# Input rows of token groups 1 to 3 scaled in a channel-by-token layout instead of being transposed on TensorE, and a reordered start of the kernel

## The chip, the cores and the metric

The kernel runs on one core of one Trainium2 chip. The core's engines run their own instruction streams in order and wait for each other through semaphores: TensorE (PE in the profile, with PEld for its weight loads), VectorE (DVE), ScalarE (ACT), GpSimd (POOL) and SyncE (SP). DMA transfers are issued from the streams of SP, ACT and POOL. The metric is the time of one execution on the device in microseconds (us), lower is better. Before the change it is 1321.57 us, the median of 3 runs (1318.48 to 1323.26).

## The reference, cut to what matters

One layer of an encoder, 2048 tokens of width 1024, all in float32. The change touches only the first two lines: the modulated RMS norm that makes `h`, and the part of the input projection that is computed first.

```
c_act = silu(c)
shift, scale, gate = split(c_act @ w_ada + b_ada, 3)
h = rmsnorm(x, norm_w) * (1 + scale) + shift          # x: 2048 tokens x 1024 channels
proj = h @ w_in + b_in                                # 1024 -> 4624 columns
...                                                   # 2-D neighbourhood attention, bidirectional mLSTM
out = rmsnorm(x + gate * (mixed @ w_out), final_norm_w)
```

For one token `t` and one channel `d` this is `h[t, d] = x[t, d] * r[t] * g[d] + s[d]`, where `r[t]` is the reciprocal root of the mean square of the token's row, `g` is `norm_w * (1 + scale)` and `s` is `shift`.

## The kernel before

The tokens are worked on in four **groups** of 512 (`NG`, `GT`), a group in four tiles of 128 tokens. The channels are eight **slices** of 128 (`KT`, index `k`). TensorE contracts over the partitions, so `h` has to lie with channels on the partitions and tokens along the free dimension: tile `hhi[g][:, k, :]` for the high part in fp32r and `hlo[g][:, k, :]` for what that rounding leaves over. Every product is made of three: high by high, high by low and low by high (`mm3`, lines 560 to 562).

The input `x` comes as rows of tokens. `square` (line 253) sums the squares of a row on ScalarE, `roots` makes `r` with a few small VectorE steps, `scale_x` multiplies the row tile by it, and TensorE transposes the 128x128 pieces into PSUM (`turned` for group 0, line 357; `make_h` for groups 1 to 3, line 372). From PSUM, `make_h` makes the high part on ScalarE (line 374), the full value on VectorE (line 376) and the low part on GpSimd (line 377).

All this stands in `start` (with `vo_first` and `vo_group`, which it calls) under a manual schedule: each engine runs its instructions in the order in which the code emits them. The order is:

1. **The front.** Loads of group 0's rows, of the conditioning vector spread over 128 partitions (`cb`, 512 KB), of modulation weights (`load_mod`) and of projection weights (`load_p`). TensorE runs 20 products on constants (`dense`, line 329), which serve nothing but keeping it busy. Then it makes `g` and `s` of slice 0 (line 349); those of the other slices are dot products on VectorE (`mod`, line 257).
2. **The k loop** over the eight slices of group 0. For each, ScalarE makes the high part and the full value (`first_h`, line 364), VectorE the low part (line 365) and the next slice's two dot products, and TensorE runs 24 products (`products`, line 392) into `firsts` (block 0, four PSUM banks of the pool `pp`) and `seconds` (block 1, two banks). In the last two slices ScalarE also squares group 1's rows, and a third block's weights are split into `w_extra` (lines 212 and 213).
3. **Evictions and block 2 of group 0.** `vo_group` adds the bias on VectorE while it copies a PSUM bank to a staging tile (line 632), takes a sigmoid of one half on ScalarE (line 638) and stores the tile to DRAM (`d_ck`, lines 641 and 643). There are two staging tiles, used in turn, so the third call needs the store of the first to have landed.
4. **Groups 1 to 3**: `vo_first(g)` runs block 0 slice by slice (line 615, 12 products of 272 columns per slice, 96 in all) into the four banks of `pp`, and `vo_group(1, 1, g)` then runs block 1, 24 products of 256 columns for each of the four token tiles.

Between the token tiles of such a `vo_group` stands `next(self.chain)`, which emits the next group's preparation: after the third tile's eviction (o = 2) come slices 0 and 1 of `make_h`, after the fourth's (o = 3) slices 2 and 3, then slice 4; slices 5 to 7 follow the first three slices of the next `vo_first`:

```
def next_h(tiles):
    yield
    yield
    for k in (0, 2):
        make_h(tiles, k)
        make_h(tiles, k + 1)
        yield
```

## Time and profile before

| | |
|---|---|
| median of 3 runs | 1321.57 us |
| the profiled execution's own time | 1321.6 us |
| its span, first to last instruction | 1319.8 us |
| mean granted TensorE clock | 0.993 of full speed |
| bytes moved | 257.59 MB, 195 GB/s over the span |
| first product of the projection | 18.11 us |
| first eviction of block 0: groups 1, 2, 3 | 78.81, 105.77, 132.71 us |

A row of the timeline gives the start, the duration, the engine, the source line, the operation and its tiles; in brackets stands how long the engine had been idle and what ended that. Rows with xN are N instructions merged, from the first's start to the last's end. A row of windows gives each engine's busy time in a stretch (and its instructions in parentheses), then the granted TensorE clock, the busy share of the DMA engines and their rate. A TensorE product in float32 shows as two instructions. Matmuls overlap in their pipeline, so the distance from one start to the next is what a product costs, not its duration. Everything the change touches lies in the first 135 us.

### The profile page before, as it was taken

The page shows a single profiled execution, that of the slowest core. Times are in us where ns is not written, and L with a number is a line of the kernel's source. Part 1 is how long each engine was busy: PE and PEld are TensorE (multiplying, and loading weights), DVE is VectorE, ACT ScalarE, POOL GpSimd, SP SyncE. Part 2 cuts the span into 40 slices and gives each one's busy share as a digit, 9 for nine tenths or more (in the row PEclk, how much of TensorE's full clock was granted, in tenths as well). Part 3 has the DMA queues.
Part 4 walks back from the last instruction along what each step waited for, and adds up shares of the span by engine and source line. Part 5 has one row for each costly group of instructions (what it writes and reads, how often), then busy time and mean ns, then how long its engine had stood idle before and what let it go on. Part 6 is the DMA issues. An engine that isn't in the chain of part 4 may idle for free.

```text
span 1319.8 us, 23211 instructions
## 1 busy us (share of the span) xinstructions
PE 1287.2 (98%) x8244; PEld 1106.7 (84%) x8244; DVE 784.7 (59%) x2418; ACT 540.4 (41%) x1175; POOL 223.6 (17%) x279
## 2 busy tenths in 40 slices
PE   9899999999999999999999999999999999999996
PEld 8899999999888787888888888888777778778785
DVE  6754542113456577266778788777547676666663
ACT  5543423543313423123323333333356555465561
POOL 0044102442000000111222002121211211112211
PEclk9999999999999999999999999999999999999999
DMA  9967966999276786445757766746789877868871
GB/s 363 338 165 210 259 157 155 227 236 226 77 185 174 181 210 175 143 137 166 210 149 209 236 175 205 234 152 185 208 254 237 204 199 189 187 169 194 194 186 48
DMA packets 235237, 257.59 MB, mean 195 GB/s; under 512 B 30950, under 2 KB 192102, under 8 KB 235122
## 3 DMA queue, kind: packets, MB, share of 16 engines
q1 hardware_dynamic: 150174, 183.10, 49.8%
q0 software_dynamic: 20496, 36.21, 11.3%
q10 hardware_dynamic: 64452, 36.80, 10.0%
q8 instruction: 65, 1.06, 0.3%
q14 instruction: 50, 0.41, 0.1%
HBM read 171.51 MB, written 92.72 MB: 200 GB/s over the span
## 4 chain that ended last, share of the span: by engine, by line
PE 80%; DMA 8%; DVE 5%; issue 3%; ACT 2%; POOL 0%; ACTq 0%; SPq 0%; DVEq 0%; POOLq 0%
PE pq L1003 21%; PE y L1582 11%; PE pc L560 4%; PE pc L561 4%; PE pc L562 4%; PE pvo L560 3%; PE pvo L562 3%; PE pvo L561 3%; PE pT L1522 3%; DMA tab<-d_t 3%; PE pO L1537 3%; PE pvo L615 3%; PE pv L562 2%; PE pv L561 2%; PE pv L560 2%
## 5 line engine op out<-in xcount | busy, mean ns | idle before, releaser
L1003 PE MATMUL pq<-hhi,whi_a 128*128 128x512 f32 x512 | 208.2, 407 | 0.8 <-ACT u L908 0.8
L1003 PE MATMUL pq<-hlo,whi_a 128*128 128x512 f32 x512 | 208.3, 407 | 0.0
L1003 PE MATMUL pq<-hhi,wlo_a 128*128 128x512 f32 x512 | 206.7, 404 | 0.0
L1003 PEld LDWEIGHTS pq<-hhi,whi_a 128*128 128x128 f32 x512 | 96.8, 189 | 17.7 <-ACT u L908 1.3
L1003 PEld LDWEIGHTS pq<-hhi,wlo_a 128*128 128x128 f32 x512 | 96.8, 189 | 16.4
L1003 PEld LDWEIGHTS pq<-hlo,whi_a 128*128 128x128 f32 x512 | 96.7, 189 | 16.0 <-issue 0.5
L1524 ACT ACTIVATE pt<-pT 96x384 f32<-96x384 f32 (+3 forms) x128 | 65.9, 515 | 88.2 <-PE pT L1522 85.3
L1503 ACT ACTIVATE pbuf<-pbuf,mn 128x480 f32<-128x480 f32 (+5 forms) x128 | 76.1, 596 | 51.7 <-DVE mn L1502 51.5
L977 POOL TENSOR_TENSOR wlo_a<-rawq,whi_a 128x1024 fp32r<-128x1024 f32 x19 | 45.5, 2397 | 290.2 <-ACT whi_a L976 276.8
L1582 PE MATMUL y<-hhi,whi_a 128*128 128x512 f32 x256 | 91.3, 418 | 1.0 <-ACT whi_a L1552 1.0
L1582 PE MATMUL y<-hhi,wlo_a 128*128 128x512 f32 (+1 forms) x272 | 91.6, 403 | 0.2 <-ACT y L1589 0.2
L1502 DVE CUSTOM_DVE_ANT_0 pbuf<-pS,tab 128x480 f32<-128x480 f32 (+5 forms) x128 | 63.2, 540 | 39.6 <-PE pS L1494 33.0
L1247 ACT ACTIVATE num<-px,gtile 128x129 f32<-128x129 f32 x120 | 38.3, 366 | 113.8 <-PE px L1242 86.2
L1522 PEld LDWEIGHTS pT<-ident,pbuf 128*128 128x128 f32 (+2 forms) x416 | 51.2, 137 | 28.7 <-issue 8.7
L1522 PE MATMUL pT<-ident,pbuf 128*128 128x128 f32 (+2 forms) x416 | 67.7, 276 | 7.2 <-DVE pbuf L1514 5.7
L1266 POOL TENSOR_TENSOR hm<-hm,ck 128x128 f32<-128x128 f32 x64 | 26.5, 414 | 255.2 <-DVE hm L1265 229.5
L632 DVE TENSOR_TENSOR stvo<-pvo,brow 128x256 f32<-128x256 f32 x60 | 24.9, 423 | 75.3 <-PE pvo L562 57.2
L560 PE MATMUL pvo<-whi_b,hhi 128*128 128x256 f32 x224 | 63.8, 285 | 0.0
L850 ACT ACTIVATE dec<-dec,gtile 128x128 f32<-128x128 f32 x128 | 42.7, 394 | 50.5 <-POOL dec L843 44.6
L562 PE MATMUL pvo<-whi_b,hlo 128*128 128x256 f32 x224 | 63.0, 281 | 0.0
L561 PE MATMUL pvo<-wlo_b,hhi 128*128 128x256 f32 x224 | 63.0, 281 | 0.0
L1582 PEld LDWEIGHTS y<-hhi,wlo_a 128*128 128x128 f32 x272 | 48.7, 191 | 9.0 <-issue 2.4
(331 smaller groups left out, 3374.3 us busy)
## 6 DMA issues: line engine op xcount, KB each, us to landing
ck<-d_ck SPq DMA_DIRECT2D x64, 384.5 KB
rawq<-in_w_main_dram SPq DMA_DIRECT2D x28, 512.0 KB
raw<-in_w_main_dram SPq DMA_DIRECT2D x18, 512.0 KB
kv<-d_ck SPq DMA_DIRECT2D x64, 128.5 KB
dec<-d_mneg SPq DMA_DIRECT2D x32, 256.0 KB
d_ck<-dec ACTq DMA_DIRECT2D x32, 256.0 KB
d_qna<-qst ACTq DMA_DIRECT2D x32, 256.0 KB
xr<-in_x_dram POOLq DMA_DIRECT2D x15, 512.0 KB, 8.6
```

Of the source, the lines that this page charges most:

```text
L560: nc.tensor.matmul(ps, lhi(k), rhi(k), start=(k == 0), stop=False)
L561: nc.tensor.matmul(ps, lhi(k), rlo(k), start=False, stop=False)
L562: self.mark = nc.tensor.matmul(ps, llo(k), rhi(k), start=False, stop=(k == KT - 1))
L615: self.nc.tensor.matmul(self.firsts[o][:, :272], h, (hi, lo, hi)[n][:, k, :], start=(k == 0 and n == 0), stop=(k == KT - 1 and n == 2))
L850: nc.scalar.activation(t[:, o, :], t[:, o, :], AF.Exp, bias=self.cols["g"][:, d, h, c : c + 1])
L977: (eng or nc.gpsimd).tensor_tensor(lo[:, :, cs], raw, hi[:, :, cs].bitcast(F32), ALU.subtract)
L1003: self.mark = nc.tensor.matmul(patch_ps(ps) if patch else ps, w, self.htok(h, g, k, patch), start=(k == 0 and n == 0), stop=(k == KT - 1 a ...
L1502: nc.vector.tensor_tensor_reduce(pt[:, :nk], ps, tabs[place[u]][j][:, :nk], 1.0, 3e38, ALU.add, ALU.min, mn)
L1503: nc.scalar.activation(pt[:, :nk], pt[:, :nk], AF.Exp, bias=mn, scale=-1.0, accum_out=sums[:, j : j + 1])
L1522: nc.tensor.transpose(ps[:cs, i, :], U[u][j][:, i * cs : (i + 1) * cs], self.ident)
L1524: nc.scalar.activation(t[:cs, :nch, :], ps[:cs, :nch, :], AF.Copy)
L1582: nc.tensor.matmul(y, m[:, k, :], w[k][:, cs], start=(k == 4 and n == 0), stop=(k == 3 and n == 2))
```

## The change

**Groups 1 to 3.** The host hands over a second copy of `x`, `x_t`, laid out by group, channel within the slice, slice, token. `make_h` no longer transposes: `load_t` brings the group's channels straight in. The rows are still loaded, for their sums of squares only, so 6 MB are read in addition. The factor `r[t]`, which now runs along the free dimension, is spread over all partitions by `spread`: four small VectorE steps put it on diagonals, and four float32 products with a matrix of ones (128 columns each) write it to a PSUM bank. A slice of `h` is then a VectorE step (x by `g` by the bank), ScalarE's high part with the shift, and a VectorE step for the low part; GpSimd has no part in it.

**The front.** The conditioning vector is loaded as one row on ScalarE's queue, ahead of its three small loads; ScalarE takes its silu, TensorE spreads it with two float32 products of 512 columns and ScalarE copies it out. These two products stand ahead of the constant ones, which are now 14, with 3 and 2 more around the second half of the sums for slice 0. Group 0's rows are scaled in two pieces. The modulation weights are loaded earlier.

**The end of the k loop.** The last slice's products run bank by bank, group 1's rows are loaded in slice 6 instead of slice 2 and squared after the loop instead of within it, and the first two tiles of block 2 of group 0 go to two banks of another pool (`tops`).

```
@@ start
-            nc.sync.dma_start(t, self.x[tt * P : (tt + 1) * P, :])
+        def load_t(g):
+            held = self.hpools[g + 1].tile([P, 4, D], F32, tag=f"hhi{g + 1}", name=f"xt_{g}") if g < 3 else None
+            for j in range(4):
+                t = x_tile(f"xt_{g}_{j}") if held is None else held[:, j, :]
+                nc.sync.dma_start(t, self.x_t[g, :, 2 * j : 2 * j + 2, :].rearrange("p k t -> p (k t)"))
+                for i in range(2):
+                    xc[g, 2 * j + i] = t[:, i * GT : (i + 1) * GT]
...
+        def spread(tiles, rst):
+            diag = xp.tile([P, GT], F32, tag="h", bufs=2, name=f"diag_{tiles[0]}").rearrange("p (j q) -> p j q", j=4)
+            for j in range(4):
+                nc.vector.tensor_scalar(diag[:, j, :], self.ident, rst[:, j : j + 1], None, ALU.mult)
+            ps = self.tq.tile([P, GT], F32, tag="tb", name=f"rb_{tiles[0]}")
+            def run():
+                for j in range(4):
+                    nc.tensor.matmul(ps[:, j * P : (j + 1) * P], self.ones, diag[:, j, :], start=True, stop=True)
+            return ps, run
...
+        crow = ada.tile([1, D], F32, name="crow")
+        nc.scalar.dma_start(crow, self.c_row)
-        nc.sync.dma_start(cb, self.c_row.broadcast_to([P, D]))
...
-        for _ in range(20):
-            nc.tensor.matmul(dense[:, :240], self.ident, self.big, start=True, stop=True)
+        nc.scalar.activation(crow, crow, AF.Silu)
+        for j in range(2):
+            cbs.append(self.tq.tile([P, GT], F32, tag="tp", name=f"cb_{j}"))
+            nc.tensor.matmul(cbs[j], self.ones[0:1, :], crow[:, j * GT : (j + 1) * GT], start=True, stop=True)
+        warm(14)
...
         def make_h(tiles, k):
-            tp = self.tq.tile([P, GT], F32, tag=("tp", "tb")[k % 2], name=f"tp_{tiles[0]}_{k}")[:, :n]
-            for j, tt in enumerate(tiles):
-                nc.tensor.transpose(tp[:, j * P : (j + 1) * P], xt[tt][:, k * P : (k + 1) * P], self.ident)
-            nc.scalar.activation(hi, tp, AF.Identity, bias=self.shT[:, k : k + 1], scale=self.gT[:, k : k + 1])
-            nc.vector.tensor_scalar(h, tp, self.gT[:, k : k + 1], self.shT[:, k : k + 1], ALU.mult, ALU.add)
-            nc.gpsimd.tensor_tensor(lo, h, hi.bitcast(F32), ALU.subtract)
+            nc.vector.scalar_tensor_tensor(h, xc[g, k], self.gT[:, k : k + 1], spreads[g], ALU.mult, ALU.mult)
+            nc.scalar.activation(hi, h, AF.Identity, bias=self.shT[:, k : k + 1])
+            nc.vector.scalar_tensor_tensor(lo, h, self.shT[:, k : k + 1], hi.bitcast(F32), ALU.add, ALU.subtract)
...
         def products(k):
             turns = [(b, o, n) for ns in ((0, 1), (2,)) for b in range(2) for o in range(4) for n in ns]
+            if k == KT - 1:
+                turns.sort()
...
-        def next_h(tiles):
+        def next_h(tiles, run):
             yield
+            run()
             yield
             for k in (0, 2):
...
-                self.vo_group(2, 2, 0, brow=brow)
+                tops = [self.tq.tile([P, GT], F32, tag="tp", name=f"pvo_2_{o}") for o in range(2)]
+                self.vo_group(2, 2, 0, brow=brow, tops=tops)
```

Three places show how instructions move. The first is VectorE's order where group 2 is prepared during block 1 of group 1: `pvo` are the banks being evicted to the staging tile `stvo`, `h` and `hlo` the slices made for group 2. Before:

```order
L632 TENSOR_TENSOR stvo_1_994<-pvo_6_1049,brow_130 128x2x128
L376 TENSOR_SCALAR h_0_1081<-tp_0_1075,gT,shT 128x512
L376 TENSOR_SCALAR h_1_1090<-tp_1_1084,gT,shT 128x512
L632 TENSOR_TENSOR stvo_1_994<-pvo_7_1093,brow_130 128x2x128
L376 TENSOR_SCALAR h_2_1125<-tp_2_1119,gT,shT 128x512
```

The same place now:

```order
L672 TENSOR_TENSOR stvo_1_993<-pvo_6_1052,brow_130 128x2x128
L406 SCALAR_TENSOR_TENSOR h_0_1078<-xt_650,gT,rb_992 128x512
L408 SCALAR_TENSOR_TENSOR hlo_954<-h_0_1078,shT,hhi_953 128x512
L406 SCALAR_TENSOR_TENSOR h_1_1082<-xt_650,gT,rb_992 128x512
L408 SCALAR_TENSOR_TENSOR hlo_954<-h_1_1082,shT,hhi_953 128x512
L672 TENSOR_TENSOR stvo_1_993<-pvo_7_1086,brow_130 128x2x128
L406 SCALAR_TENSOR_TENSOR h_2_1112<-xt_650,gT,rb_992 128x512
L408 SCALAR_TENSOR_TENSOR hlo_954<-h_2_1112,shT,hhi_953 128x512
```

The low part of a slice, which was GpSimd's, now stands on VectorE between the full value of its slice and that of the next, and it reads `hhi`, which ScalarE makes from that full value in between.

The second place is the start of TensorE's stream, up to the first transpose. Before:

```order
L329 MATMUL dense<-big,ident 128x240 x20
L349 MATMUL mod_251<-cact,mod_hi 128x1 x16
L357 MATMUL tp_0_270<-ident,x_164 128x128
L357 MATMUL tp_0_270<-ident,x_166 128x128
L357 MATMUL tp_0_270<-ident,x_168 128x128
```

The same place now:

```order
L356 MATMUL cb_198<-crow,ones 128x512
L356 MATMUL cb_200<-crow,ones 128x512
L350 MATMUL dense<-big,ident 128x240 x14
L381 MATMUL mod_252<-cact,mod_hi 128x1 x8
L350 MATMUL dense<-big,ident 128x240 x3
L381 MATMUL mod_252<-cact,mod_hi 128x1 x8
L350 MATMUL dense<-big,ident 128x240 x2
L392 MATMUL tp_0_278<-ident,x_166 128x128
```

TensorE's first instruction now needs ScalarE's silu of the row `crow`, and five constant products stand inside the sums for slice 0.

The third place is ScalarE's order from the end of the k loop to the first store of a staging tile (`junk` are the squares of group 1's rows). Before:

```order
L253 ACTIVATE junk_550,ssq_284<-xs_383 128x1024
L253 ACTIVATE junk_552,ssq_284<-xs_383 128x1024
L212 ACTIVATE w_extra<-raw_0_344 128x1024
L364 ACTIVATE hhi_102<-tp_7_537,shT,gT 128x512
L364 ACTIVATE h_7_580<-tp_7_537,shT,gT 128x512
L253 ACTIVATE junk_584,ssq_284<-xs_383 128x1024
L253 ACTIVATE junk_586,ssq_284<-xs_383 128x1024
L212 ACTIVATE w_extra<-raw_1_511 128x1024
L638 ACT_TABLE_LOAD
L638 ACTIVATE stvo_0_635<-stvo_0_635 128x4x128
L641 DMA d_ck<-stvo_0_635 128x4x257
```

The same place now:

```order
L212 ACTIVATE w_extra<-raw_0_353 128x1024
L399 ACTIVATE hhi_102<-tp_7_541,shT,gT 128x512
L399 ACTIVATE h_7_588<-tp_7_541,shT,gT 128x512
L212 ACTIVATE w_extra<-raw_1_515 128x1024
L260 ACTIVATE junk_630,ssq_629<-x_554 128x1024
L260 ACTIVATE junk_632,ssq_629<-x_556 128x1024
L260 ACTIVATE junk_634,ssq_629<-x_558 128x1024
L260 ACTIVATE junk_636,ssq_629<-x_560 128x1024
L678 ACT_TABLE_LOAD
L678 ACTIVATE stvo_0_660<-stvo_0_660 128x4x128
L681 DMA d_ck<-stvo_0_660 128x4x257
```

All four squares now stand between the second weight split and the table load ahead of the first sigmoid and its store.

130 lines of the change are left out of this document (71 added, 59 removed).

## The prediction

> **What bounds the kernel now.** I read the page's totals and chain first, then windows over the changed part, then its timeline. TensorE is the bound:
>
> ```profile
> span 1319.8 us, 23211 instructions
> PE 1287.2 (98%) x8244; PEld 1106.7 (84%) x8244; DVE 784.7 (59%) x2418; ACT 540.4 (41%) x1175; POOL 223.6 (17%) x279
> ...
> PE 80%; DMA 8%; DVE 5%; issue 3%; ACT 2%; POOL 0%; ACTq 0%; SPq 0%; DVEq 0%; POOLq 0%
> ```
>
> ```profile
> 20.00:30.00 10.00, 9.62 (x79) 9.26 (x77) 9.74 (x16) 4.83 (x8) 0.00 (x0) 0.99 1.03 404
> 40.00:50.00 10.00, 7.83 (x60) 7.17 (x58) 6.94 (x12) 9.58 (x15) 0.00 (x0) 1.00 0.90 327
> 50.00:60.00 10.00, 8.70 (x62) 8.73 (x63) 6.83 (x26) 4.24 (x5) 0.00 (x0) 0.83 0.97 336
> 90.00:100.00 10.00, 10.00 (x86) 10.00 (x85) 6.16 (x9) 5.22 (x8) 8.09 (x7) 1.00 0.87 238
> ```
>
> Columns: PE, PEld, DVE, ACT, POOL, clock, DMA. In the k loop (20 to 30) VectorE is as full as TensorE, 9.74 of 10. Around 50 TensorE idles and its clock falls. From 60 on it is never idle. So taking TensorE work out of groups 1 to 3 pays only while the engines that feed it keep up, and whatever the third group's end is shifted by, the 98% busy remainder passes on. I therefore follow three marks, the first eviction of block 0 in groups 1, 2 and 3:
>
> ```profile
> 78.81 0.43 DVE L632 TENSOR_TENSOR stvo<-pvo,brow 128x256 f32<-128x256 f32 x1 [4.71 <-PE pvo L615]
> ...
> 88.49 0.43 DVE L632 TENSOR_TENSOR stvo<-pvo,brow 128x256 f32<-128x256 f32 x1 [2.42 <-PE pvo L562]
> ...
> 105.77 0.43 DVE L632 TENSOR_TENSOR stvo<-pvo,brow 128x256 f32<-128x256 f32 x1 [4.71 <-PE pvo L615]
> ...
> 132.71 0.43 DVE L632 TENSOR_TENSOR stvo<-pvo,brow 128x256 f32<-128x256 f32 x1 [4.71 <-PE pvo L615]
> ```
>
> A group takes 26.95 us, all of it TensorE issuing.
>
> **Groups 2 and 3: what goes and what comes.** Gone are 32 transposes a group:
>
> ```profile
> 92.01 1.47 PE L372 MATMUL tp<-ident,xs 128*128 128x128 f32 x12
> 93.24 0.37 PE L615 MATMUL pvo<-whi_a,hhi 128*128 128x272 f32 x1
> ```
>
> Twelve of them hold the next product off by 1.23, and it settles 0.09 later: 0.11 each, 3.5 us a group. Added are four float32 products of 128 columns. The constant products, 240 columns and two records each, give the rate:
>
> ```profile
> 1.50:6.20 4.70, 4.63 (x12) 3.94 (x13) 1.00 0.95 329
> 6.60:12.40 5.80, 5.73 (x29) 5.03 (x27) 1.00 0.97 331
> ```
>
> That is 0.40 a record at first and 0.20 later, so 0.11 for 128 columns: eight records, 0.9, with weight loads 1.0 us. If nothing waited, a group would gain 2.5.
>
> But VectorE now runs full value, low part, full value, low part, and each low part waits for ScalarE's high part of the same slice, which waits for the full value. VectorE takes its instructions in order, so a slice costs a whole round:
>
> ```profile
> L945 DVE SCALAR_TENSOR_TENSOR acc_k<-u,cw,acc_k 128x512 f32<-128x512 f32 x64 | 45.5, 747 | 0.4
> ...
> L1038 DVE SCALAR_TENSOR_TENSOR qst<-pq,bcol,qst 128x512 fp32r<-128x512 f32 x24 | 17.9, 747 | 18.4 <-ACT qst L1037 18.4
> ...
> L947 ACT ACTIVATE acc_k<-acc_k,cb 128x512 f32<-128x512 f32 x16 | 11.6, 722 | 12.8 <-DVE acc_k L945 12.8
> ...
> L299 ACT ACTIVATE whi_a<-raw 128x512 fp32r<-128x512 f32 x4 | 2.5, 629 | 0.7 <-DMA raw<-in_w_main_dram 0.7
> ...
> 157.28 1.41 DVE L529 SCALAR_TENSOR_TENSOR gsum<-ga,cact,gsum 128x512 f32<-128x512 f32 x2
> ```
>
> The fused step of 512 columns takes 0.747, from SBUF (L945) or with a PSUM operand (L1038); two in a row start 0.66 apart (L529). ScalarE from SBUF takes 0.63 as a plain copy and 0.72 with a bias column, which is this case. The hand-over costs 0.03 (45.53 + 0.77 to 46.33, below). Round: 0.75 + 0.03 + 0.72 + 0.03 + 0.66 = **2.2 us**, bounds 2.1 and 2.3. TensorE eats a slice of block 0 in 1.5 (12 products 0.125 apart). Before, GpSimd took the low parts and kept ahead:
>
> ```profile
> 101.14 1.30 POOL L377 TENSOR_TENSOR hlo<-h,hhi 128x512 fp32r<-128x512 f32 x1 [0.44 <-DVE h L376]
> ```
>
> Its last low part ended 13.95 after the third eviction (88.49), in good time for the last slice. Now: third eviction 0.34, two rounds 4.4, fourth eviction 0.34 (it waits behind those rounds, and the next block needs its bank), six rounds 13.2 and 0.1 to the end: the last low part comes 18.4 after the third eviction starts. Ten products behind it and the drain make 1.4: block 0 ends **19.8** after that eviction. Unhindered it would be one tile (2.85) and 96 products (12.1), so some 4.9 are waiting.
>
> From the end of block 0 to the next third eviction TensorE needs three tiles (8.55), the spread (1.0) and a drain: 9.6. The roots lie beside this:
>
> ```profile
> 80.47 0.16 DVE L263 TENSOR_SCALAR ssq<-ssq 128x4 f32<-128x4 f32 x1
> ...
> 82.64 2.74 DVE L272 TENSOR_SCALAR xs<-xs,rst 128x1024 f32<-128x1024 f32 x4
> ```
>
> From the first small step to the scaling is 2.2. After ScalarE's four squares (4.8 behind the last high part, 1.19 each, rows further down) VectorE makes the roots in 2.2 and the diagonals in 0.6 (four steps like the small ones), and has them 5.5 after the block's end, when the second tile's products end at 5.75. If that cover is lost, the spread starts later by the difference. A group takes 9.6 + 19.8 = 29.4 instead of 26.95: **+2.45 each, +4.9** for groups 2 and 3. With rounds of 2.1 and 2.3 it is +3.3 and +6.5.
>
> [...]
>
> **The front.** The rows it rests on:
>
> ```profile
> 1.57 10.76 PE L329 MATMUL dense<-big,ident 128*128 128x240 f32 x40 [1.57 <-POOL stvo L621]
> 1.67 0.45 ACTq L305 DMA_DIRECT2D nw<-in_norm_w_dram  x1
> 2.16 1.28 ACT L332 ACT_TABLE_LOAD   x1 [2.16 <-issue]
> ...
> 9.71 1.06 ACT L338 ACTIVATE c_all<-c_all 128x1024 f32<-128x1024 f32 x1 [1.33 <-DMA c_all<-in_c_row_dram]
> ...
> 12.81 3.70 PE L349 MATMUL mod<-cact,mod_hi 128*128 128x1 f32 x32 [0.48 <-DMA mod_hi<-in_w_mod_dram]
> ...
> 17.29 0.78 ACT L364 ACTIVATE hhi<-tp,shT,gT 128x512 fp32r<-128x512 f32 x1 [0.23 <-PE tp L357]
> ...
> 18.11 0.59 PE L392 MATMUL pvo<-whi_a,hhi 128*128 128x272 f32 x1
> ```
>
> TensorE began at 1.57. Now its first product needs a silu that comes after four DMA issues (one more, 0.45), the table load (1.28) and 1.06 for 1024 columns: 5.0. Two products of 512 columns are four records of 0.85 at the half rate, to 8.4. The rate doubled 4.9 after the start; so again at 9.9, with four of the 28 constant records done; 24 at 0.20 end at 14.8. Sums 3.7, five constant products 2.0, transposes 0.44, high part 0.8: the first product at 21.8, or 20.3 if the rate doubles after 1.9. I take 21.1, **+3.0**; the bounds are -2 (the sums only wait for their weights, which are now loaded ahead of 768 KB that came first before) and +5 (the clock falls during the sums). The weights aren't late: TensorE waits for them no longer. [...]
>
> Since VectorE is full in the loop and its first low part waits for this, the delay stays, less 0.3 that ScalarE gains without the squares: +2.7 at the loop's end.
>
> **The end of the loop and group 1.**
>
> ```profile
> 45.53 0.77 ACT L364 ACTIVATE h<-tp,shT,gT 128x512 f32<-128x512 f32 x1
> 46.19 1.05 ACT L253 ACTIVATE junk<-xs 128x1024 bf16<-128x1024 f32 x1
> 46.33 0.69 DVE L365 TENSOR_TENSOR hlo<-h,hhi 128x512 fp32r<-128x512 f32 x1
> ...
> 47.37 1.06 ACT L253 ACTIVATE junk<-xs 128x1024 bf16<-128x1024 f32 x1
> ...
> 48.42 1.04 ACT L212 ACTIVATE w_extra<-raw 128x1024 fp32r<-128x1024 f32 x1
> ...
> 51.30 0.55 PE L560 MATMUL pvo<-w_extra,hhi 128*128 128x256 f32 x1 [2.42 <-DVE gates L634]
> ...
> 52.33 0.64 ACT L638 ACTIVATE stvo<-stvo 128x512 f32<-128x512 f32 x1 [1.56 <-DVE stvo L632]
> 53.04 0.40 ACTq L641 DMA_DIRECT2D d_ck<-stvo  x1
> ...
> 62.09 1.09 DVE L632 TENSOR_TENSOR stvo<-pvo,brow_x 128x256 f32<-128x256 f32 x3 [4.88 <-DMA d_ck<-stvo]
> ```
>
> Here the change helps TensorE: the 2.42 wait goes, and with it the low clock after it (0.83 over the ten microseconds from 50, 1.7 lost at most; I take 1.3). The last slice now waits for its low part (47.0) and runs 22 products, to 49.7, or 52.4 with the delay; its third tile of block 2 ends at 62.0 with the spread. But that is not what comes last. VectorE's evictions of block 2 wait for the first staging tile's store, 9.05 after its issue at 53.04. That issue now stands behind all four squares: split to 47.3, four squares of 1.19 to 52.1, table load 1.28, sigmoid 0.64, with the delay 56.8. The store shares the DMA engines with group 2's rows; I take 8 to 9 (bounds 6 and 10): 65.3, third eviction near **65.5**. Plus 19.8: block 0 of group 1 ends at 85.3, **+6.5** on 78.81.
>
> Sum: +6.5 + 4.9 = **+11.4** on the profiled execution's 1321.6, which equals the median: **1333**.
>
> **Rivals.**
> - *TensorE's work decides throughout.* If a round fitted into 1.5, the change would save 10.6 of transposes, pay 3 for spreads and gain 2.9 at the loop's end: 1311. The idle 90 to 100 of VectorE (6.16 busy) speaks for it; the in-order round of 2.2 against it. It would need the fused step and ScalarE both a third faster than any row.
> - *The front and the store are no later.* Group 1's third eviction would come when TensorE's third tile is done, near 59.3 without the delay: 79.1, +0.3, and +4.9 or, at 2.1 a round, +3.3: 1325 to 1327. A front two earlier than now: 1323.
> - *The added 6 MB.* The DMA engines are 0.97 busy from 50 to 60 already. If channel tiles or the store land 5 us later than I have them, group 1 starts that much later: 1338 and more. It decides once the store takes over 10.
>
> **Chances.** Forecast (1326 to 1339) 0.70; front and store not late, 1318 to 1326, 0.13; TensorE decides, 1311 to 1317, 0.11; DMA, over 1339, 0.06. A difference within 0.3% (4 us) cannot be told from none. Faster 0.11, same 0.13, slower 0.76. Range 1321 to 1339: it leaves out the faster case, the lower part of the second and most of the last.
>
> **What would show it.** Right: in groups 2 and 3 the fused steps alternate about 2.2 apart, TensorE shows waits for `hlo` of 0.5 to 0.7 a slice in block 0, and marks lie 29 to 30 apart; the first product after 20; the third eviction of block 2 ended by the store's landing. Wrong: marks 24 to 25 apart, low parts ending ahead of their slices, or the first product before 18.

## The result: 1.5% slower, 2 us beyond the predicted range

The changed kernel takes 1341.31 us (median of 4 runs, 1338.58 to 1342.37), the kernel before on the same chip 1322.41 (4 runs, 1318.48 to 1324.94). The ratio is 1.0146, with a 95% interval of 1.0129 to 1.0164. The forecast was 1333, with a range of 1321 to 1339: the direction, the round on VectorE and the wait for the store held; the clock at the start did not, and with it the size. The profiled execution takes 1341.4 us.

The page of the changed kernel, its totals and the shares of its chain:

```profile
span 1339.3 us, 23091 instructions
PE 1290.9 (96%) x8174; PEld 1103.9 (82%) x8174; DVE 796.4 (59%) x2447; ACT 537.9 (40%) x1176; POOL 194.3 (15%) x255
...
PE 66%; DMA 12%; DVE 8%; issue 7%; ACT 5%; POOL 1%; SPq 1%; ACTq 0%; DVEq 0%; POOLq 0%
```

TensorE's share of the chain fell from 80% to 66%; DMA, issuing, VectorE and ScalarE took it over. The three marks, in the timeline of VectorE:

```profile
91.53 0.43 DVE L672 TENSOR_TENSOR stvo<-pvo,brow 128x256 f32<-128x256 f32 x1 [0.54 <-PE pvo L655]
...
121.01 0.43 DVE L672 TENSOR_TENSOR stvo<-pvo,brow 128x256 f32<-128x256 f32 x1 [0.55 <-PE pvo L655]
...
150.43 0.43 DVE L672 TENSOR_TENSOR stvo<-pvo,brow 128x256 f32<-128x256 f32 x1 [0.54 <-PE pvo L655]
```

They are 12.7, 15.2 and 17.7 later than before; the span is 19.5 longer. So 12.7 are lost up to the first mark, 2.5 in each of the next two groups, and 1.8 behind the third (the span from that mark to the end, the **remainder**, is 1188.9 instead of 1187.1).

**Up to the first mark.** First the start of TensorE's timeline:

```profile
5.08 3.78 PE L356 MATMUL cb<-crow,ones 1*128 1x512 f32 x4 [5.08 <-ACT crow L352]
8.79 8.87 PE L350 MATMUL dense<-big,ident 128*128 128x240 f32 x28
17.50 1.84 PE L381 MATMUL mod<-cact,mod_hi 128*128 128x1 f32 x16
19.20 1.46 PE L350 MATMUL dense<-big,ident 128*128 128x240 f32 x6
20.50 2.40 PE L381 MATMUL mod<-cact,mod_hi 128*128 128x1 f32 x16
22.77 1.95 PE L350 MATMUL dense<-big,ident 128*128 128x240 f32 x4
24.50 1.91 PE L392 MATMUL tp<-ident,x 128*128 128x128 f32 x8
26.49 0.60 PE L426 MATMUL pvo<-whi_a,hhi 128*128 128x272 f32 x1
```

TensorE starts at 5.08 (predicted 5.0) but reaches the first product at 26.49 (predicted 21.1, before 18.11). The 28 constant records take 8.71 up to the sums: at the 0.40 and 0.20 a record of before's constants that is, by estimate, 15.6 slow ones, so the rate doubled near 15.0, where 9.9 was predicted. (The clock column of the windows still reads 1.00 for this first slow stretch, from 7.96 to 11.37 for one, so only the distances of the records show it.) Then it fell again, as the windows of the next stretch show (columns as in the prediction: the clock is the third number from the end):

```profile
18.18:21.60 3.42, 3.42 (x28) 3.35 (x27) 0.16 (x2) 0.00 (x0) 0.00 (x0) 1.00 1.04 407
21.60:25.01 3.41, 3.41 (x14) 3.05 (x14) 0.00 (x0) 0.50 (x2) 0.00 (x0) 0.50 1.02 402
25.01:28.42 3.41, 3.33 (x15) 2.93 (x14) 1.27 (x3) 2.76 (x5) 0.00 (x0) 0.50 1.04 405
```

The stretch ahead of the fall holds the end of the first sums, six constant records and half of the second sums, and TensorE is busy for all of it: it is not idleness that lowered the clock. Next the end of the k loop, where the forecast had the first store issued at 56.8 and the third eviction at 65.5: the timeline of ScalarE's queue with that issue, then that of VectorE, then the ten microseconds from 70 as a window:

```profile
62.15 0.39 ACTq L681 DMA_DIRECT2D d_ck<-stvo  x1
```

```profile
71.97 1.09 DVE L672 TENSOR_TENSOR stvo<-pvo,brow_x 128x256 f32<-128x256 f32 x3 [8.45 <-DMA d_ck<-stvo]
72.97 0.74 DVE L406 SCALAR_TENSOR_TENSOR h<-xt,gT,rb 128x512 f32<-128x512 f32 x1
74.49 0.75 DVE L408 SCALAR_TENSOR_TENSOR hlo<-h,shT,hhi 128x512 fp32r<-128x512 f32 x1 [0.79 <-ACT hhi L407]
75.16 0.74 DVE L406 SCALAR_TENSOR_TENSOR h<-xt,gT,rb 128x512 f32<-128x512 f32 x1
76.69 0.75 DVE L408 SCALAR_TENSOR_TENSOR hlo<-h,shT,hhi 128x512 fp32r<-128x512 f32 x1 [0.79 <-ACT hhi L407]
```

```profile
70.00:80.00 10.00, 5.26 (x33) 4.84 (x32) 5.67 (x11) 2.16 (x3) 0.21 (x2) 0.81 0.71 240
```

The issue is 5.35 later than predicted, as much as the first product. The store takes 9.69 (in the chain of waits), and all three evictions of block 2 stand behind it, the third at 72.64. TensorE is busy for only 5.26 of the ten microseconds. The four VectorE rows are the round: low parts 2.20 apart, each with 0.79 of waiting for ScalarE, as predicted (2.2).

### The profile page after: what moved, and what is told of

Read it like the earlier page. It is cut to its first block, busy times and chain, and to the rows that moved or that the text cites. A ratio compares the mean times of both kernels' runs of the same rounds, so it can differ in the third digit from the quotient of the medians.

```text
span 1339.3 us, 23091 instructions
## 1 busy us (share of the span) xinstructions
PE 1290.9 (96%) x8174; PEld 1103.9 (82%) x8174; DVE 796.4 (59%) x2447; ACT 537.9 (40%) x1176; POOL 194.3 (15%) x255
## 4 chain that ended last, share of the span: by engine, by line
PE 66%; DMA 12%; DVE 8%; issue 7%; ACT 5%; POOL 1%; SPq 1%; ACTq 0%; DVEq 0%; POOLq 0%
PE pq L1043 18%; PE y L1622 11%; PE pc L601 4%; PE pc L600 4%; PE pc L602 4%; DMA tab<-d_t 3%; PE pT L1562 3%; PE pO L1577 2%; PE pS L1534 2%; DMA dec<-d_mneg 2%; PE pvo L600 2%; PE pvo L601 2%; PE pvo L602 2%; PE px L1282 2%; PE pi L1284 2%
## 5 line engine op out<-in xcount | busy, mean ns | idle before, releaser
L1562 PEld LDWEIGHTS pT<-ident,pbuf 128*128 128x128 f32 (+2 forms) x416 | 50.9, 137 | 30.0 <-issue 10.5
L635 DVE TENSOR_TENSOR stv<-pv,brow 128x256 f32<-128x256 f32 x32 | 12.8, 422 | 72.7 <-PE pv L602 47.0
```

The source lines that it names most:

```text
L1562: nc.tensor.transpose(ps[:cs, i, :], U[u][j][:, i * cs : (i + 1) * cs], self.ident)
```

## The experiments

Each run has its own runs of the kernel before beside it, so ratios are compared. "Value stage" is the stretch from the first load of a decay tile (`dec`) to the last eviction of the two value blocks (`stv`, whose staging tiles go to `d_vna`); in before it ends 188.0 us behind the third mark. All numbers but the ratios are from each run's one profile; that execution can lie some us off the median (e4 and e12 4 above it, e11 7 above, e14 4 and e16 10 below). e3 has only two runs. The last two columns are the longest wait of a VectorE eviction there for a store (VectorE's idle time before it), and TensorE's wait for a bank there.

| kernel | ratio to before (95%) | marks 1, 3 | mark 3 to end of value stage | longest store wait | TensorE waits |
|---|---|---|---|---|---|
| before | 1 | 78.81, 132.71 | 188.0 | 8.8 | 0 |
| changed | 1.0146 (1.0129 to 1.0164) | 91.53, 150.43 | 190.4 | 11.0 | 0.6 |
| e1 front of before | 1.0134 (1.0106 to 1.0162) | 84.05, 142.94 | 198.8 | 16.8 | 6.4 |
| e2 constants first | 1.0169 (1.0135 to 1.0203) | 89.08, 147.97 | 195.5 | 14.9 | 4.4 |
| e3 128 rows | 1.0197 (1.0163 to 1.0230) | 91.13, 150.02 | 195.7 | 14.4 | 4.0 |
| e4 low parts one behind | 1.0111 (1.0082 to 1.0140) | 88.00, 136.74 | 197.8 | 14.0 | 5.1 |
| e5 before, 6 MB more | 1.0001 (0.9984 to 1.0019) | 78.85, 132.75 | 188.0 | 8.4 | 0 |
| e6 4 MB less | 1.0115 (1.0091 to 1.0138) | 88.14, 147.16 | 193.2 | 13.4 | 3.0 |
| e7 e4 and e6 | 0.9999 (0.9984 to 1.0014) | 79.06, 127.79 | 189.0 | 10.1 | 0 |
| e8 e1 and e4 | 1.0058 (1.0042 to 1.0075) | 80.40, 129.13 | 196.4 | 13.1 | 3.9 |
| e9 e1, tables early | 1.0121 (1.0098 to 1.0145) | 84.20, 143.09 | 192.6 | 10.3 | 0 |
| e10 e8, tables early | 1.0059 (1.0029 to 1.0090) | 77.46, 130.79 | 196.1 | 11.1 | 0.6 |
| e11 e8, squares late | 1.0052 (1.0033 to 1.0071) | 81.67, 130.40 | 199.2 | 14.7 | 7.3 |
| e12 e11, tables early | 1.0086 (1.0063 to 1.0109) | 81.91, 130.65 | 197.1 | 8.8 | 0 |
| e13 e1 and e6 | 1.0097 (1.0073 to 1.0122) | 79.67, 138.70 | 198.2 | 16.1 | 6.5 |
| e14 e1, e4 and e6 | 1.0009 (0.9990 to 1.0027) | 74.47, 123.20 | 198.1 | 13.8 | 5.3 |
| e15 sums from channel tiles | 1.0162 (1.0134 to 1.0189) | 74.69, 140.13 | 200.3 | 14.4 | 7.7 |
| e16 e1, decay loads moved | 1.0199 (1.0160 to 1.0238) | 84.59, 143.50 | 201.2 | 13.0 | 7.3 |
| e17 e8, decay loads moved | 1.0098 (1.0069 to 1.0128) | 77.94, 126.67 | 207.6 | 13.0 | 9.1 |
| e18 before, decay loads moved | 1.0084 (1.0062 to 1.0106) | 78.64, 132.57 | 197.4 | 13.4 | 4.0 |

In the row of the changed kernel the 11.0 is the following wait. The profile puts it down to TensorE, but all four banks were full by then, as the four evictions in one go show; the store that had to land first was issued at 297.56:

```profile
305.89 1.42 DVE L635 TENSOR_TENSOR stv<-pv,brow 128x256 f32<-128x256 f32 x4 [11.04 <-PE pv L602]
```

### The front: e1, e2, e3

e1 puts the front of before into the changed kernel (the front's part of the diff above, backwards, with the old order of loads). e2 and e3 change one thing each:

```
e2: the constants ahead of the spreading products
+        warm(14)
         for j in range(2):
             cbs.append(...)
             nc.tensor.matmul(cbs[j], self.ones[0:1, :], crow[:, j * GT : (j + 1) * GT], start=True, stop=True)
-        warm(14)
e3: 128 rows instead of one
-        crow = ada.tile([1, D], F32, name="crow")
+        crow = ada.tile([P, D], F32, name="crow")
+        nc.gpsimd.memset(crow, 0.0)
...
-            nc.tensor.matmul(cbs[j], self.ones[0:1, :], crow[:, j * GT : (j + 1) * GT], start=True, stop=True)
+            nc.tensor.matmul(cbs[j], self.ones, crow[:, j * GT : (j + 1) * GT], start=True, stop=True)
```

> The changed kernel with the front of before (conditioning vector loaded spread over 128 partitions, silu on 128 partitions, 20 constant products first, none inside the sums, loads in the old order); the rest as changed. Theory (the front is what was mis-sized: first product 26.49 us instead of 18.11, and VectorE, full in the k loop, passes all of it on): first product near 18.1, first store issued near 54 instead of 62.15, first mark (first eviction of block 0 in group 1) near 83.5 instead of 91.53, the distance between marks still 29.4, whole kernel 8 us less than changed, near 1333. Rival (the front's delay is hidden in the loop and the squares or the added loads make the first mark late): first product near 18.1 but first mark still above 88 and at most 3 us gained, 1338 or more.

> The changed kernel with the 14 constant products ahead of the two products that spread the conditioning vector, so TensorE has work at once; all else as changed. Theory (TensorE's late start and the half clock during the constants make most of the 8.4): TensorE starts near 1.6, its rate has doubled by 8.4 at the latest, first product between 18 and 21 (above 20 where the rate falls again within the sums), first mark 5 to 8 below 91.53, kernel 1333 to 1336. Rival (the sums' weights or the load order make the first product late, not TensorE's own rows): first product stays above 24, kernel within 2 us of 1341.

> The changed kernel with the two spreading products contracted over 128 rows instead of one (127 of them zero; the row's load waits for the zeros, about 1 us). [...] Whole kernel under theory 1 to 3 us less than changed or, as the row comes about 1 later, no different; under the rival 1 us more.

e1: first product 18.88, first store issued at 54.39, first mark 84.05, groups 29.45. Up to the third mark the theory holds to under a microsecond, and yet the time is that of the changed kernel: the 7.5 are lost again in the value stage, to which the later runs turn.

e2 and e3 show the clock. TensorE's timeline in e2, then two windows of e2, then TensorE's timeline in e3:

```profile
1.56 7.39 PE L350 MATMUL dense<-big,ident 128*128 128x240 f32 x28 [1.56 <-POOL stvo L661]
8.89 1.98 PE L357 MATMUL cb<-crow,ones 1*128 1x512 f32 x4
10.80 3.08 PE L381 MATMUL mod<-cact,mod_hi 128*128 128x1 f32 x16
```

```profile
7.96:11.37 3.41, 3.41 (x14) 1.82 (x14) 1.84 (x4) 1.05 (x2) 0.00 (x0) 1.00 1.02 392
11.37:14.79 3.42, 3.42 (x16) 3.29 (x16) 2.56 (x14) 1.80 (x5) 0.00 (x0) 0.50 0.92 321
```

```profile
7.13 3.57 PE L357 MATMUL cb<-crow,ones 128*128 128x512 f32 x4 [7.13 <-ACT crow L353]
10.54 5.83 PE L351 MATMUL dense<-big,ident 128*128 128x240 f32 x28
```

In e3 all 28 constants take 0.20 a record, so the rate had doubled by 10.5, within 3.4 us of the first spreading product; in the changed kernel, where these products have one row, it took 9.9 from there. So in these two runs single-row products did not raise the clock and the same products over 128 rows did, which e3 was to tell apart. In e2 the rate doubles during the constants, which start at 1.56 (8.6 slow records by the same estimate, doubled near 5.0), but a window that holds the last constants, the spreading products and the first sums, busy for all its 3.41, is followed by half rate, which lasts to 25.0: first product 23.28, outside the 18 to 21 expected. The whole times were expected below 1341 (e2) and no higher than it (e3) and came out at 1346 and 1351. Part of that is the value stage again, with 4.4 and 4.0 of waiting; in e3 nearly 6 us more than in the changed kernel lie behind it.

### The round on VectorE: e4

```
             nc.scalar.activation(hi, h, AF.Identity, bias=self.shT[:, k : k + 1])
-            nc.vector.scalar_tensor_tensor(lo, h, self.shT[:, k : k + 1], hi.bitcast(F32), ALU.add, ALU.subtract)
+            low_h()
+            lows.append(lambda: nc.vector.scalar_tensor_tensor(lo, h, self.shT[:, k : k + 1], hi.bitcast(F32), ALU.add, ALU.subtract))
```

`low_h` emits the low part that was put aside last; the last one follows slice 7.

> The changed kernel with the low part of a slice put behind the full value of the next slice on VectorE (groups 1 to 3), nothing else moved. Theory (the in-order round of 2.2 us on VectorE is what costs 4.9 a group): the two fused steps follow each other 0.67 apart, low parts come about 1.4 to 1.6 apart, TensorE sets the pace, distance between marks 24.5 to 25.5 instead of 29.45, marks earlier by 4, 9 and 13 to 14, and the weights of the third block (7.27 after their issue, 1.7 us of TensorE waiting behind the third mark) come earlier against their use; kernel 1325 to 1328, 13 to 16 less than changed. Rival (ScalarE's high part or the evictions in VectorE's stream set the pace, not the round): marks 27 or more apart, kernel 1334 or more.

VectorE in group 2, with the mark of that group as the last row:

```profile
104.58 0.75 DVE L406 SCALAR_TENSOR_TENSOR h<-xt,gT,rb 128x512 f32<-128x512 f32 x1
105.25 0.75 DVE L409 SCALAR_TENSOR_TENSOR hlo<-h,shT,hhi 128x512 fp32r<-128x512 f32 x1
...
106.03 0.75 DVE L406 SCALAR_TENSOR_TENSOR h<-xt,gT,rb 128x512 f32<-128x512 f32 x1
106.70 0.74 DVE L409 SCALAR_TENSOR_TENSOR hlo<-h,shT,hhi 128x512 fp32r<-128x512 f32 x1
...
112.37 0.43 DVE L679 TENSOR_TENSOR stvo<-pvo,brow 128x256 f32<-128x256 f32 x1 [1.15 <-PE pvo L662]
```

No wait is left between the steps, low parts come 1.45 apart, and a group takes 24.37: the 4.9 a group that the prediction put down to waiting are gone, and this is 2.6 less than before. The third mark is 13.7 earlier than in the changed kernel. The time gains a third of a per cent only, where 13 to 16 us were expected; the value stage ends 197.8 behind the mark, and some 8 us more than in before are lost behind that stage.

### The bytes: e5, e6, e7, e8

```
e5: the kernel before, row tiles loaded once more into a tile that nobody reads, in three places
+                nc.sync.dma_start(again[:, j, :], self.x[(4 * g + j) * P : (4 * g + j + 1) * P, :])
e6: the changed kernel without rows of groups 2 and 3
-        load_x(2)
...
-        load_x(3)
...
+                if g < 3:
+                    xt[4 * g + 4 + j] = t
```

e7 is e4 with this edit, e8 is e1 and e4 together.

> The kernel before, with 6 MB more to load and nothing else: twelve row tiles (groups 1 to 3, 512 KB each) are loaded a second time into a tile that nobody reads, where the changed kernel loads its channel tiles. Theory (up to 320 us the DMA engines are a second bound, and the added 6 MB by themselves cost what the changed kernel loses): marks within 2 us of 78.81, 105.77 and 132.71, but the last eviction of the value blocks, 320.69 in before, 10 to 20 later with TensorE waiting for stores behind 280; kernel 1332 to 1342. Rival (55 us of idle DMA engines up to 240 take them in, and the loss is on VectorE and in the front): that eviction within 4 of 320.69, kernel 1321 to 1327.

> The changed kernel without the rows of groups 2 and 3, 4 MB less: ScalarE's sums of squares for these groups read the channel tile of the group before instead, as many squares of the same size; the roots of groups 2 and 3 are therefore of other numbers. The first store has less beside it. Theory (third mark and DMA engines are two bounds, and the later of them counts; in the changed kernel they lie within 1 us of each other): third mark 145 to 150 as the store lands up to 5 earlier, remainder behind the mark 1187 to 1189, kernel 1333 to 1339. Rival A (DMA alone decides): 1322 to 1328. Rival B (the marks alone, and the rows have no part in them): 1340 to 1342.

> The last two together: low parts one slice behind on VectorE, and no rows of groups 2 and 3 (roots of groups 2 and 3 of other numbers). Theory (two bounds): third mark 131 to 137, and what the interleaved kernel lost behind it (its remainder was 1204.6 against 1187.1 of before, 7.5 of it between 260 and 320) is gone, remainder 1187 to 1191: kernel 1320 to 1328, 11 to 18 less than the interleaved one's 1338.7. Rival (what was lost behind the mark has nothing to do with the bytes, but with where the stores stand in the queue): remainder 1198 or more, kernel 1332 or more.

> The front of before and the low parts one slice behind, both in the changed kernel, with all its loads. Theory (two bounds): third mark near 129, 21 earlier than the changed kernel's 150.43 and 3.5 earlier than before's 132.71, but the DMA engines hold the value blocks back: the last of their evictions not before 330 (before 320.69), kernel 1333 to 1341. Rival (the marks decide): remainder 1187 to 1192, kernel 1317 to 1322.

e5 refutes that 6 MB cost anything by themselves in the kernel before: all marks and the end of the value stage stay within 0.1. In e6 the first store, issued at 62.13, lets the evictions go at 67.06:

```profile
67.06 0.76 DVE L672 TENSOR_TENSOR stvo<-pvo,brow_x 128x256 f32<-128x256 f32 x2 [3.54 <-DMA d_ck<-stvo]
69.24 0.43 DVE L672 TENSOR_TENSOR stvo<-pvo,brow_x 128x256 f32<-128x256 f32 x1 [1.42 <-PE pvo L602]
```

So the store takes about 4.9 where group 2's rows do not share the DMA engines with it, and 9.7 where they do; TensorE is what the third eviction waits for then, and the marks gain 3.3. e7 is level with the kernel before, though its third mark is 4.9 earlier. e8 reads all rows, has its third mark 3.6 earlier than before and is 0.6% slower: its value stage takes the difference. The times of e6 and e7 fit the theory of two bounds (e7's third mark is earlier than its 131 to 137); e8, with its last eviction at 325.6 and a time between the two forecasts, meets neither theory nor rival, and e13 and e14 will go against the theory.

### The squares and the tables: e9 to e12

```
e11: group 1's squares behind the first stores
-        for _ in sums_x(range(4, 8)):
-            pass
...
                 self.vo_group(1, 1, 0, seconds)
+                for _ in sums_x(tiles):
+                    pass
e9, e10, e12: the tables' preparation ahead of the third mark, 48 of its stores on GpSimd's queue
-            nc.sync.dma_start(self.d_e[ct][:, i, :, start - k0 : start - k0 + 16], self.d_rneg[:, :, dx : dx + 16])
+            nc.gpsimd.dma_start(self.d_e[ct][:, i, :, start - k0 : start - k0 + 16], self.d_rneg[:, :, dx : dx + 16])
...
+                    self.tables_begin()
...
+            if g:
+                self.tables_columns(g - 1)
```

> The changed kernel with the front of before (as in the first experiment, whose third mark was 7.5 earlier and whose time was no less), and with the preparation of the bias tables (the small loads and stores that fill d_rneg and d_e, 48 of them with rows of 64 bytes) moved ahead of the third mark, on GpSimd's queue, instead of behind it on SP's. Theory (the stage of the value blocks, 72 to 190 us behind the third mark, has full DMA engines and no slack, so what stands late in it took the front's gain): third mark near 143, last eviction of the value blocks 187 to 191 behind it instead of 198.8, kernel 1331 to 1336. Rival (the front's gain is lost to something that the tables have no part in, as the bytes are the same): that eviction again 195 or more behind the mark, kernel 1339 or more.

> The front of before, the low parts one slice behind, and the tables' preparation ahead of the third mark; all loads of the changed kernel. Theory: third mark near 129 as without the tables' move, last value eviction 187 to 191 behind it instead of 196.4, kernel 1316 to 1322, below the kernel before or level with it. Rival (bytes decide): 195 or more behind the mark, kernel 1326 or more.

> The front of before and the low parts one slice behind, and the four squares of group 1 behind the sigmoids of group 0's first two staging tiles instead of ahead of them; the tables as changed. Theory (the first store, issued behind the squares, sets the third eviction of block 2): first store issued 4 to 5 earlier, near 50 instead of 55, third mark 3 to 5 earlier than 129.1; but the value blocks take most of it: last value eviction 195 or more behind the mark, kernel 1324 to 1329. Rival A (TensorE's third tile or the squares' own lateness sets it): third mark within 1 of 129. Rival B (no loss behind the mark): kernel 1318 to 1323.

> All four: front of before, low parts one slice behind, squares behind the first stores, tables' preparation ahead of the third mark. Theory: third mark 124 to 126, last value eviction 187 to 191 behind it, kernel 1312 to 1318, faster than both kernels. Rival (a bound of the DMA engines by bytes): no faster than 1322.

In all three runs with early tables TensorE's wait in the value stage is gone (6.4 to 0, 3.9 to 0.6, 7.3 to 0) and the longest store wait is 8.8 to 11.1. But the waiting moved. In e10 it is for ScalarE's high parts ahead of the third mark and for the third block's weights and the gates' small steps behind it, in e12 for diagonals and weights: in TensorE's waits up to 340 us, the weights of the third block cost 4.5 and 2.0, the diagonals 4.3.

e9's value stage ends 6.2 earlier behind the mark, e12's 2.1, e10's 0.3; e9's time is 0.1% lower with overlapping intervals, the other two times are no lower. e9, e10 and e12 were expected 3 to 22 us faster than they are. e11 issues the first store at 52.05 instead of 55.10, and the mark does not gain: with the squares behind it, group 1's diagonals come late and the spread waits 3.6 for them. That is the mechanism of its rival A, though the mark comes 1.3 later than e8's, where within 1 was expected.

### Where the front's gain goes: e13 to e18

e13 is e1 with the edit of e6, e14 is e8 with it. e15 computes everything without the rows of groups 2 and 3:

```
+                nc.scalar.activation(sq[:, j, :], xp2[g, j], AF.Square)
...
+                        nc.gpsimd.tensor_tensor(acc, last, part, ALU.add)
...
+                nc.tensor.matmul(ps[:, j : j + 1], accs[g][:, j * P : (j + 1) * P], self.ones[:, 0:1], start=True, stop=True)
```

e16, e17 and e18 change the queue of the 32 decay loads, in e1, e8 and before:

```
-            self.behind(nc.sync.dma_start(t, src.broadcast_to([P, 512])), self.mark)
+            self.behind(nc.gpsimd.dma_start(t, src.broadcast_to([P, 512])), self.mark)
```

> The changed kernel with the front of before and without the rows of groups 2 and 3 (the sums of squares for these groups read the channel tile of the group before, so their roots are of other numbers). Two earlier runs bear on it: the front of before alone brought the third mark 7.5 forward and no time; less bytes alone brought 3.3 at the mark and 4. Theory (the transfers that the 6 MB push behind the third mark are what ate the front's gain): both gains come through, third mark near 139.5, last eviction of the value blocks 188 to 191 behind it (198.8 with the front of before and all rows), kernel 1327 to 1331. Rival (that stage costs 195 and more whenever the marks come earlier than the changed kernel's, whatever the bytes): kernel 1334 or more.

> As the run before, and the low parts one slice behind on VectorE. Theory: third eviction of block 2 near 60.5 (store issued near 55, five long), groups of 24.4, third mark 121 to 125, last value eviction 188 to 191 behind it, kernel 1311 to 1316, faster than before by half a per cent. Rival (as above): 195 or more behind the mark, kernel 1319 or more.

> A version that computes everything and reads no rows of groups 2 and 3: front of before, low parts one slice behind, and for groups 2 and 3 the squares are of the channel tiles (four ScalarE steps as before), GpSimd adds the eight slices (seven steps of 512 columns, near 1.3 each, 9 a group, beside block 0), and four products with one column of ones, behind the first tile of block 1, give the sums per token, from which the roots follow as now. Theory: third mark 121 to 127, 1 to 2 a group lost where the roots now come after the first tile, remainder as in the run before, kernel 1311 to 1319, faster than before. Rival (the sums come too late for the spread, or GpSimd beside VectorE stretches the fused steps): groups of 27 or more, third mark 129 or more, kernel 1320 or more.

> The changed kernel with the front of before, and the 32 loads of the decay tiles (dec, 256 KB each) issued from GpSimd's queue instead of SP's; all bytes as they were. Theory (order, not bytes: in the stage of the value blocks the stores of the staging tiles, d_vna, stand on SP behind loads of decay tiles that wait for a free buffer; SP stood 6.36 us in that wait ahead of the store that held TensorE up for 6.4): the wait of TensorE there is gone, last value eviction 187 to 191 behind the third mark instead of 198.8, kernel 1331 to 1335 against 1342 with the front of before alone. Rival (the DMA engines are full and the order does not matter): 195 or more, kernel 1339 or more.

> Front of before, low parts one slice behind, decay loads on GpSimd's queue; everything computed, all rows loaded. Theory (order): third mark near 129, last value eviction 187 to 191 behind it (196.4 with the loads on SP), kernel 1317 to 1322, level with the kernel before or up to 5 less. Rival (bytes): 195 or more behind the mark, kernel 1326 or more.

> The kernel before with only the decay loads on GpSimd's queue, as the control. Both theories: TensorE waits for nothing in the value blocks of before, so no change, 1319 to 1324; slower if GpSimd, in order, holds the loads back behind its additions of the mask.

e13 and e14 have their third marks where they were expected (138.70 and 123.20), and the rival holds: the value stage ends 198 behind the mark with 4 MB less, too. e14's third mark is 9.5 earlier than before, and its time is the same. e15 fails on its own terms: TensorE waits 4.6 a group for GpSimd's additions, and its groups take 32 to 33. e18, the control, makes e16 and e17 useless for the question of order: the move lengthens the store waits in before itself, to 13.4, and costs 0.8%.

What the lost time consists of is shown by e1. The waits of VectorE in before (total, times, longest), the waits of both engines in e1, and a window of e1:

```profile
DVE stv L595 <- DMA d_vna<-stv: 23.1, 4, 8.8
```

```profile
DVE stv L617 <- DMA d_vna<-stv: 55.7, 6, 16.8
...
PE pv L582 <- DVE stv L617: 6.4, 1, 6.4
```

```profile
302.45:309.28 6.83, 4.30 (x20) 4.31 (x21) 1.42 (x4) 2.34 (x5) 2.53 (x2) 0.50 1.05 275
```

An eviction that waits for a store holds one bank; the pool has four, and TensorE fills one in 2.84 (evictions at 280.22 and 283.06 in the changed kernel), so by this estimate it can run on for 11.4 at most. The table keeps to that limit: with a longest store wait up to 10.3 TensorE does not wait, at 11.0 and 11.1 it waits 0.6, from 13.0 on 3 to 9. Before lies at 8.8, 2.2 short of the first loss. And the wait costs more than itself: after e1's 6.4 of idling the clock is at half rate for 6.8 us, and TensorE works in 4.3 of them, which is up to 2.2 more. With 1.4 of waiting in the third block, right behind the third mark, that makes 10.0, and e1's value stage ends 10.8 later behind the mark than before's.

Why the stores come late can be read from SP's queue, though no experiment settles it. A staging tile is full after four evictions, and SP then issues its store. The fourth eviction of the third tile and the issue of its store, in before, in the changed kernel and in e1:

```profile
263.76 0.43 DVE L595 TENSOR_TENSOR stv<-pv,brow 128x256 f32<-128x256 f32 x1 [2.42 <-PE pv L562]
275.97 0.41 SPq L600 DMA_DIRECT2D d_vna<-stv  x1
```

```profile
283.06 0.43 DVE L635 TENSOR_TENSOR stv<-pv,brow 128x256 f32<-128x256 f32 x1 [2.42 <-PE pv L602]
297.56 0.39 SPq L640 DMA_DIRECT2D d_vna<-stv  x1
```

```profile
275.89 0.42 DVE L617 TENSOR_TENSOR stv<-pv,brow 128x256 f32<-128x256 f32 x1 [2.42 <-PE pv L584]
290.29 6.36 SPq L861 DMA_DIRECT2D dec<-d_mneg  x3
296.74 1.01 SPq L622 DMA_DIRECT2D d_vna<-stv  x1
```

The issue comes 11.8, 14.1 and 20.4 after the tile is full, and from there the next eviction into that tile starts 7.4, 8.3 and 7.8 later. So the store itself is hardly slower; it is issued later, in e1 directly behind three decay loads that SP takes 6.36 to issue (6.16 in the changed kernel). In all 20 profiles the latest of the first six stores is issued up to 15.3 after its tile is full where TensorE waits 0.6 or less, and 16.7 or more where it waits 3 or more. And SP keeps its own time: e1 has its tile ready 7.2 earlier than the changed kernel and issues the store at 296.74 instead of 297.56, the next two at 309.31 and 318.92 instead of 309.33 and 319.10. That is where e1's gain goes.

## Why the prediction was off

- **The round and the groups: right.** Rounds of 2.20 (predicted 2.2), groups of 29.48 and 29.42 (29.4), +2.5 each (+2.45); e4 shows the cause, as the loss goes with the round.
- **The front: the step that failed.** "So again at 9.9, with four of the 28 constant records done" took over the 4.9 us of before's start, and "Sums 3.7, five constant products 2.0" counted on full rate. The front cost 8.4 instead of 3.0, beyond even the upper bound of 5. The clock was at half rate up to 15.0 and again from 21.6 to 28.4: products of one row did not raise it (doubled 9.9 after the first of them, in e3, with 128 rows, within 3.4), and a window filled largely with one-column sums did not hold it up (18.18 to 21.60, TensorE busy for all 3.42 of it, 0.50 behind it). Against the sum, the constants took 2.3 more, the sums with their five products 1.3, transposes and high part 0.8, the spreading products 0.3; another 0.7 is that 21.1 was taken where the sum gave 21.8. No row shows the doubling after 1.9 that the other value, 20.3, stood on; it came 9.9 after TensorE's start. The rows of before had a hint that was not used: after its sums the clock fell for 3.41 us, though TensorE never idled:

```profile
13.29:16.70 3.41, 3.41 (x32) 3.41 (x33) 1.61 (x4) 1.39 (x3) 0.00 (x0) 1.00 1.04 410
16.70:20.11 3.41, 3.41 (x16) 2.81 (x14) 2.18 (x5) 2.32 (x5) 0.00 (x0) 0.50 1.05 407
```

- **That the front's delay stays: right as a step.** First product and first store are both 5.4 later than predicted.
- **The store: mechanism right, 1.2 short.** 9.69 against 8.5, within the bounds of 6 and 10; e6 shows that sharing makes half of it. The rival of the added bytes was to decide "once the store takes over 10": it did not get there, and e5 shows that the bytes alone cost nothing. So its number, 1338 and more, came out by another way than it said.
- **From the third eviction to the mark: 18.9 instead of 19.8.** The evictions queue up behind the store, so the third starts 0.7 later than the store allows, which nearly makes up for it.
- **"The 98% busy remainder passes on": nearly right for this change, wrong as a rule.** Behind the third mark 1188.9 against 1187.1; 1.1 of the 1.8 are idling in the third block, whose weights took 7.27 from issue in the chain of waits, and 0.6 are in the value stage. In the experiments the remainder was up to 22 longer than before's (e4: 17.5), in part by the value stage's limit (9.8 of e4's), in part behind that stage, where the runs were not taken apart.

The sum for the changed kernel: 5.4 (front), 1.2 (store), 0.6 and -0.9 (evictions, block 0), 0.1 (groups), 1.8 (behind) make 8.2 of the 8.4 by which the profiled execution exceeds 1333. This says where the time of this execution lies, not what a shorter front would have saved: e1 has the front of before and is no faster, 1.0134 against 1.0146 with overlapping intervals.

**What stays open.** Why SP issues the value blocks' stores hardly earlier when the marks come earlier, with the same order of instructions behind the front (e1 above; e14's third store goes at 276.31, before's at 275.97, though e14's third mark is 9.5 earlier). By the view of its waits SP waits there mostly for the stores of the decay tiles (`d_ck`) to land, for 62.7 of 101.4 us of waits in e1 between 150 and 345; in e18, whose decay loads are on another queue, the stores are issued up to 27 late all the same, so those loads are not all that holds SP. The number of bytes does not decide it alone: 4 MB less gained 0.3 to 1.1% in each of four pairs (e6, e7, e13, e14), yet the value stage of e13 and e14 still ends 198 behind the mark. The tables' small stores have a part in it, as TensorE's wait goes with them (e9, e10, e12), but moving them brought other waits. The order of SP's queue could not be tested cleanly (e18). No version that computes everything beat the kernel before; the best, e8, is 0.6% slower.

## What to carry to other kernels

Where one engine makes both a value and its low part, and a second engine works between them, write the low part of the last piece behind the value of the next: here that took 5.1 us off a group. Before a delay or a gain is passed on through a busy remainder, look in the later stages for waits that a buffer only just covers, and compare the longest wait with the cover (here 8.8 with an estimated 11.4 at most): a gain upstream can be lost there whole. Where an eviction waits for a store, look at when the store was issued before blaming the transfer. Do not count on products of one row or one column to keep the clock up: here the rate doubled only 9.9 us after the first single-row product, and it halved behind a busy window of 3.41 us that held mostly single-column sums (before, at 16.70).

## What the runs showed of the hardware

- Products contracted over one row did not raise TensorE's clock, although it was busy without a gap: doubled 9.9 us after the first of them, against at most 3.4 with 128 rows, 127 of them zero (e3). After a window filled almost wholly with single-column sums it fell (before, at 16.70), and after one of single-row products with some constants and sums too (e2, at 11.37).
- The stretches at half rate quoted here are multiples of 3.41 us: 3.41 in before (from 16.70), 6.83 in the changed kernel (from 21.60), 13.65 in e2 (from 11.37). The first three falls of the changed kernel, at 21.60, 55.73 and 76.21, lie 34.13 and 20.48 apart, which is 10 and 6 times 3.41.
- A 512 KB store took 9.7 us beside loads of rows and about 4.9 without most of them (e6).
